# Max unpooling on one core: the load of x issued from ACT's queue instead of SP's

## The chip, the cores and the metric

The kernel runs on one core of a Trainium2 chip. The metric is the device time of one execution in microseconds (us), measured from outside the program; a profiled execution also has a span, the time from its first to its last recorded instruction. Less is better.

The engines that matter here are VectorE (DVE in the profile), which computes, SyncE (SP), which issues DMAs and waits, ScalarE (ACT), which in this kernel computes nothing, and the core's sixteen DMA engines, which carry all transfers between the chip's main memory (HBM) and the on-chip memory (SBUF).

## The reference

Each input value goes to one of the four places of a 2 x 2 block of the output, chosen by its index; the other three are zero.

```python
batch, channels, h, w = 16, 64, 32, 32      # x float32, indices 0..3
output = np.zeros((batch, channels, 2 * h, 2 * w), dtype=np.float32)
for b, c, i, j in all_of(x):
    idx = indices[b, c, i, j]
    output[b, c, 2 * i + idx // 2, 2 * j + idx % 2] = x[b, c, i, j]
```

x has 4.19 MB, the output 16.78 MB. The indices come to the device as 64-bit integers, 8.39 MB; the kernel reads the low 32 bits of each.

## The kernel before

The 1024 images (batch times channels) of 32 x 32 values are laid out so that each of the 128 partitions holds `T = 8` whole images one after another, which in HBM are one contiguous run for each partition. Everything fits into SBUF at once: `x_t` (32 KB a partition), `idx_t` (64 KB) and the output in groups of `G = 2` images (32 KB a partition), `NG = 4` groups in all. The fourth group uses the first group's buffer again (L94).

There are seven DMAs, each over all 128 partitions. Three are loads: the first three images' indices (L110, 24 KB a partition, `cut` marks their end), all of x (L114, 32 KB), and the other five images' indices (L116, 40 KB). Four are stores, one for each group (L151, 32 KB). Before the change all seven are issued from SP.

The order of work is written out by hand. The class `Program` puts instructions into the program's opening block: `first` places a DMA before the first drain of the engine that issues it, so that the loads go out before the engines' opening barrier, each engine's in the order of the calls; `last` moves SP's closing wait to the end of the program.

VectorE waits for x (L121) and for the first indices (L126, again before image 3 for the second indices). Then for each of the four places of the block it runs one instruction (L138) that compares the indices with the place's number and multiplies by x; the result goes with stride two into the output tile, so that the four instructions fill all of it, zeros included. The images 0 to 3 are done one at a time (instructions of 1024 elements a partition), the images 4 and 5, and 6 and 7, in pairs (2048 elements). The last instruction of a group raises the semaphore `made`, on which SP waits before it issues the group's store (L150, L151). Before the fourth group VectorE waits for the first store to have landed (L133). SP waits for the last three stores at the end (L156).

The four instructions of one image or pair:

```python
for pidx in range(4):
    op = nc.vector.scalar_tensor_tensor(
        out=o_c[:, k : k + n, :, pidx // 2, :, pidx % 2],
        in0=idx_c[:, t : t + n], scalar=pidx, in1=x_c[:, t : t + n],
        op0=mybir.AluOpType.is_equal, op1=mybir.AluOpType.mult,
    )
```

Of the kernel before, what the change touches and what calls it, by code (L numbers as in the profile page):

```python
# [1 line left out]

# [4 lines left out]

P = 128
F32 = mybir.dt.float32
I32 = mybir.dt.int32  # L10


class Program:

    def __init__(self, nc):
        self.nc = nc
        self.block = nc.main_func.blocks[0]  # L20
        self.kernel_block = nc.cur_bb.bb.name

    def __enter__(self):
        ins = self.block.instructions
        self.branches = [i for i in ins if "Branch" in type(i).__name__]
        n = len(ins) - len(self.branches)
        assert all("Branch" in type(ins[k]).__name__ for k in range(n, len(ins)))
        del ins[n:]
        self.nc.switch_bb(self.block.name, parent=None)
        self.symbolic = self.nc._always_lower_symbolic_ap  # L30
        self.nc._always_lower_symbolic_ap = False
        return self

    def first(self, made):
        ins = self.block.instructions
        assert ins[len(ins) - 1].name == made.ins.name
        moved = ins.pop()
        at = next(
            k
            for k, i in enumerate(ins)  # L40
            if i.engine == moved.engine and isinstance(i, mybir.InstDrain)
        )
        ins.insert(at, moved)

    def last(self, made):


        def move(nc):
            ins = self.block.instructions
            at = next(k for k, i in enumerate(ins) if i.name == made.ins.name)  # L50
            nc.main_func.blocks[-1].instructions.append(ins.pop(at))

        self.nc.at_finalize(move)

    def __exit__(self, kind, *_):
        self.nc._always_lower_symbolic_ap = self.symbolic
        if kind is None:
            for b in self.branches:
                self.block.instructions.append(b)
            self.nc.switch_bb(self.kernel_block, parent=None)  # L60


@with_exitstack
def kernel(
    ctx: ExitStack,
    tc: tile.TileContext,
    x: bass.AP,
    indices: bass.AP,
    kernel_size: bass.AP,
    out: bass.AP,  # L70
):
    nc = tc.nc
    assert kernel_size == 2

    B, C, H, W = x.shape
    n_img = B * C
    T = n_img // P
    assert T * P == n_img and C % T == 0

    G = 2  # L80
    NG = T // G
    FIRST = 3
    N = H * W
    x_v = x.rearrange("b (ch t) h w -> (b ch) (t h w)", t=T)
    idx_v = indices.rearrange("b (ch t) h w -> (b ch) (t h w)", t=T).bitcast(I32)
    out_v = out.rearrange("b (ch g t) oh ow -> g (b ch) (t oh ow)", g=NG, t=G)

    x_t = nc.alloc_sbuf_tensor("x_t", [P, T * N], F32).ap()
    idx_t = nc.alloc_sbuf_tensor("idx_t", [P, T * 2 * N], I32).ap()
    out_t = [  # L90
        nc.alloc_sbuf_tensor(f"out_t{g}", [P, G * 4 * N], F32).ap()
        for g in range(NG - 1)
    ]
    out_t.append(out_t[0])  # L94

    x_in = nc.alloc_semaphore("x_in")
    idx_in = [nc.alloc_semaphore(f"idx_in{g}") for g in range(2)]
    made = nc.alloc_semaphore("made")
    stored_0 = nc.alloc_semaphore("stored_0")
    stored = nc.alloc_semaphore("stored")  # L100

    x_c = x_t.rearrange("p (t i j) -> p t i j", t=T, j=W)
    idx_c = idx_t.rearrange("p (t i j two) -> p t i j two", t=T, j=W, two=2)[
        :, :, :, :, 0
    ]
    cut = FIRST * 2 * N

    with Program(nc) as program:
        program.first(
            nc.sync.dma_start(out=idx_t[:, :cut], in_=idx_v[:, :cut]).then_inc(  # L110
                idx_in[0], 16
            )
        )
        program.first(nc.sync.dma_start(out=x_t, in_=x_v).then_inc(x_in, 16))  # L114
        program.first(
            nc.sync.dma_start(out=idx_t[:, cut:], in_=idx_v[:, cut:]).then_inc(  # L116
                idx_in[1], 16
            )
        )

        nc.vector.wait_ge(x_in, 16).then_inc(x_in, -16)  # L121
        for t in range(T):
            g, k = t // G, t % G
            if t in (0, FIRST):
                half = int(t == FIRST)
                nc.vector.wait_ge(idx_in[half], 16).then_inc(idx_in[half], -16)  # L126


            if k == 1 and t != FIRST and g:
                continue  # L130
            n = 1 if k == 1 or t + 1 == FIRST or not g else 2
            if g == NG - 1:
                nc.vector.wait_ge(stored_0, 16).then_inc(stored_0, -16)  # L133
            o_c = out_t[g].rearrange(
                "p (m i two j wo) -> p m i two j wo", m=G, two=2, wo=2, j=W
# [4 lines that stand above are left out]
                    in0=idx_c[:, t : t + n],  # L140
                    scalar=pidx,
                    in1=x_c[:, t : t + n],
                    op0=mybir.AluOpType.is_equal,
                    op1=mybir.AluOpType.mult,
                )
            if k + n == G:
                op.then_inc(made, 1)

        for g in range(NG):
            nc.sync.wait_ge(made, g + 1)  # L150
            nc.sync.dma_start(out=out_v[g], in_=out_t[g]).then_inc(  # L151
                stored if g else stored_0, 16
            )
        nc.sync.sem_inc(made, -NG)
        program.last(
            nc.sync.wait_ge(stored, 16 * (NG - 1)).then_inc(stored, -16 * (NG - 1))  # L156
        )


# [1 line left out]
_INS = ['x', 'indices', 'kernel_size']  # L161
_OUTS = [((16, 64, 64, 64), 'float32')]

_NUMBERS = {'kernel_size': 2}


# [26 lines left out]
```

## Time and profile before

| | |
|---|---|
| Median of 9 runs | 71.44 us (71.39 to 71.62) |
| The profiled execution's own time | 71.43 us |
| Its span | 70.1 us |
| VectorE busy | 35.9 us, 24 instructions |
| DMA | 29.36 MB (12.58 MB read from HBM, 16.78 MB written), mean 419 GB/s over the span |
| VectorE, 1024 elements a partition | 16 instructions, 1.22 us each |
| VectorE, 2048 elements a partition | 8 instructions, 2.30 us each |

Times in the profile are microseconds from the span's start. "SPq" stands for SP's sequencer, which issues DMAs and waits; an issue's own length is the time on the sequencer, not that of the transfer. The time "to landing" of a DMA runs from its issue until the last of its sixteen completion marks has arrived, and so includes the time that it stood behind other transfers. In a table of stretches, a DMA packet counts with its whole length where it begins, so that a short stretch can show a share over 1.

### The profile page before, as it was taken

To read this page: it belongs to the slowest core of one execution; us is meant where nothing else is said; L and a number is where in the kernel's file an instruction comes from. 1 tells how busy PE (TensorE), PEld (TensorE's weight loads), DVE (VectorE), ACT (ScalarE), POOL (GpSimd) and SP (SyncE) were. 2 spreads that over 40 slices of the span, in tenths; PEclk is the share of its full clock that TensorE was granted. 3 is DMA by queue.
4 is the path that set the end of the run, shared out by engine and by line. 5 is a ranking of instruction groups with operands and counts; after the bars stand their busy time and mean duration, and the time that the engine had idled before them with its cause. 6 is when DMAs were issued, how large, how long until landed. Compare 5 with 4: busy or idle time off the path is not lost.

```text
span 70.1 us, 76 instructions
## 1 busy us (share of the span) xinstructions
DVE 35.9 (51%) x24; POOL 0.2 (0%) x4
## 2 busy tenths in 40 slices
DVE  0000000000089999999999999999999600000000
POOL 1000000000000000000000000000000000000000
DMA  8699996999988899869999696969999796969893
GB/s 224 294 393 435 449 598 299 505 393 449 524 374 374 374 561 561 374 299 505 393 393 505 299 598 299 598 299 505 393 430 467 318 580 299 598 299 524 374 449 150
DMA packets 1008, 29.36 MB, mean 419 GB/s; under 512 B 112, under 2 KB 112, under 8 KB 112
## 3 DMA queue, kind: packets, MB, share of 16 engines
q1 hardware_dynamic: 1008, 29.36, 97.8%
HBM read 12.58 MB, written 16.78 MB: 419 GB/s over the span
## 4 chain that ended last, share of the span: by engine, by line
DVE 46%; DVEq 4%; issue 1%
DVE out_t L138 46%; DVEq L188 4%
## 5 line engine op out<-in xcount | busy, mean ns | idle before, releaser
L138 DVE SCALAR_TENSOR_TENSOR out_t<-idx_t,x_t 128x1024 f32<-128x1024 int32 (+1 forms) x24 | 35.9, 1580 | 19.5 <-DVEq L126 19.5
L174 POOL MEMSET const-bfloat16-1.0<- 128x1 bf16 x1 | 0.1, 102 | 0.0
L174 POOL MEMSET const-uint8-127<- 128x1 uint8 x1 | 0.1, 102 | 0.0
L174 POOL MEMSET const-float32-0.0<- 128x1 f32 x1 | 0.1, 99 | 0.2 <-issue 0.2
L174 POOL MEMSET const-float32-1.0<- 128x1 f32 x1 | 0.1, 99 | 0.0
## 6 DMA issues: line engine op xcount, KB each, us to landing
out_dram<-out_t SPq DMA_DIRECT2D x4, 4096.0 KB, 13.4
idx_t<-in_indices_dram SPq DMA_DIRECT2D x1, 5120.0 KB, 30.5
x_t<-in_x_dram SPq DMA_DIRECT2D x1, 4096.0 KB, 18.9
idx_t<-in_indices_dram SPq DMA_DIRECT2D x1, 3072.0 KB, 9.6
```

Source lines behind the costliest of these rows:

```text
L138: op = nc.vector.scalar_tensor_tensor(out=o_c[:, k : k + n, :, pidx // 2, :, pidx % 2], in0=idx_c[:, t : t + n], scalar=pidx, in1=x_c[:, t ...
L174: nc = _bacc.Bacc("TRN2", target_bir_lowering=False, num_devices=1)
L188: with _tile.TileContext(nc) as tc:
```

## The change

The DMA that loads x is issued from ACT's queue. The two loads of indices and the four stores stay on SP's queue, in the same order as before. ACT's issue is placed, like SP's, before the engine's first drain; no wait and no semaphore changes, and nothing of VectorE's work.

```diff
         program.first(nc.sync.dma_start(out=idx_t[:, :cut], in_=idx_v[:, :cut]).then_inc(idx_in[0], 16))
-        program.first(nc.sync.dma_start(out=x_t, in_=x_v).then_inc(x_in, 16))
+        program.first(nc.scalar.dma_start(out=x_t, in_=x_v).then_inc(x_in, 16))
         program.first(nc.sync.dma_start(out=idx_t[:, cut:], in_=idx_v[:, cut:]).then_inc(idx_in[1], 16))
```

SP's issues are then: first indices, second indices, four stores. ACT's only issue is x.

## Prediction

> **What bounds the kernel now.** I read the page first, then the timeline, then the DMA issues with their times to landing, first all together and then store by store, then the DMA work in quarter-microsecond stretches at the start, and last the waits.
>
> The page says which resource is full:
>
> ```profile
> span 70.1 us, 76 instructions
> ...
> DVE 35.9 (51%) x24; POOL 0.2 (0%) x4
> ...
> DMA packets 1008, 29.36 MB, mean 419 GB/s; under 512 B 112, under 2 KB 112, under 8 KB 112
> ...
> q1 hardware_dynamic: 1008, 29.36, 97.8%
> ```
>
> VectorE works half of the span; the sixteen DMA engines are at 97.8% of it, all on one queue. The packets also tell the grain of the transfers. There are seven DMAs; 1008 packets less the 112 small ones (16 a DMA, the completion writes) leave 896, that is 128 a DMA: one packet for each partition's row, eight rows a DMA on each engine.
>
> The timeline gives the order of issue (columns: start, length, engine, line):
>
> ```profile
> 0.00 0.38 SPq L110 DMA_DIRECT2D idx_t<-in_indices_dram  x1
> ...
> 0.43 0.42 SPq L114 DMA_DIRECT2D x_t<-in_x_dram  x1
> 0.89 0.43 SPq L116 DMA_DIRECT2D idx_t<-in_indices_dram  x1
> 19.53 35.88 DVE L138 SCALAR_TENSOR_TENSOR out_t<-idx_t,x_t 128x1024 f32<-128x1024 int32 x24 [19.53 <-DVEq L126]
> 28.73 27.03 SPq L151 DMA_DIRECT2D out_dram<-out_t  x4
> ```
>
> The page's DMA issues give the time from issue to landing in their last column:
>
> ```profile
> idx_t<-in_indices_dram SPq DMA_DIRECT2D x1, 5120.0 KB, 30.5
> x_t<-in_x_dram SPq DMA_DIRECT2D x1, 4096.0 KB, 18.9
> idx_t<-in_indices_dram SPq DMA_DIRECT2D x1, 3072.0 KB, 9.6
> ```
>
> and the same view over the stretch of 28 to 30 us gives the first store alone:
>
> ```profile
> out_dram<-out_t SPq DMA_DIRECT2D x1, 4096.0 KB, 12.4
> ```
>
> Issue plus time to landing: the first indices land at 9.6, x at 0.43 + 18.9 = 19.3, the other indices at 0.89 + 30.5 = 31.4, the first store at 28.73 + 12.4 = 41.1. The same view puts the other stores, issued at 37.81, 46.62 and 55.43, at 13.0, 13.8 and 14.6, so they land at 50.8, 60.4 and 70.0. The differences are the price list: 9.7 us for x (1.21 a row on an engine), 12.1 for the second indices (1.51 a row), 9.7 a store. The first indices are three fifths of the second: 0.91 a row, 7.3 in all. Each transfer lands exactly one transfer's time after the one before. Nothing is between them: the kernel is a single file of 7.3 + 9.7 + 12.1 + 4 x 9.7 = 67.9 us, with 2.2 us of start and end, and VectorE matters only where it leaves that file without a next transfer.
>
> The DMA work at the start, in short stretches (the last two columns are DMA share and GB/s of the packets that begin there):
>
> ```profile
> 0.75:1.00 0.25, 0.00 (x0) 0.00 (x0) 1.00 0.00 0
> 1.00:1.25 0.25, 0.00 (x0) 0.00 (x0) 1.00 4.14 1081
> 1.25:1.50 0.25, 0.00 (x0) 0.00 (x0) 1.00 1.73 492
> ```
>
> The first rows begin 1.0 to 1.5 us after the issue, not on all engines at once.
>
> **The handover that matters.** The one place with little room is from loads to stores. VectorE waits for x (L121) and then for the first indices (L126):
>
> ```profile
> DVE out_t L138 <- DVEq L126: 19.5, 1, 19.5
> ```
>
> It starts at 19.53, makes the first output tile in eight instructions of 1.22 us that overlap slightly, and SP issues the first store at 28.73, 9.2 us later. A DMA from issue to landing costs 9.6 - 7.3 = 2.3 us beside its rows. The first store could have landed by itself at 28.73 + 2.3 + 9.7 = 40.7; it landed at 41.1. So the room is 0.4 us by that row. The other bound is the start row: its first packet could begin at 28.73 + 1.0 = 29.7, and the loads land at 31.4, so the room is 1.7 at most. I take 1.0, about the middle, because the 2.3 holds a first read that a busy engine may well hide in part. The later stores have more: 50.8 - (37.81 + 2.3 + 9.7) = 1.0 by the narrow row, then 1.8, then 2.6.
>
> **The change part by part.** One issue of 0.42 us leaves SP's file. SP is then free earlier: the second indices are issued at about 0.43 instead of 0.89, which is worth nothing, as they wait for two transfers on the engines; the cover is 19 us deep. The other steps that SP reaches earlier (the opening barrier) hide under VectorE's wait until 19.5 as well. ACT gains one issue; it has no other work in this kernel, nothing is queued behind it but barriers, and the price of its issue is bounded by SP's 0.38 to 0.43, all hidden. No VectorE instruction moves, no wait is added, no byte is added: 29.36 MB at the rows' prices stay 67.9 us.
>
> What really changes is the order on the engines. Before, x stood behind all of the first indices and ahead of all of the second. Now x has a queue of its own beside SP's, where both index loads follow each other. Two queues with work share an engine, and the trace of before, with one queue, doesn't show how. Bounds: if the rows alternate one by one from the start, eight rows of indices and eight of x end together, at the same 19.3: cost nothing. If x begins after SP's second row has been taken, its last row or completion write stands behind one row of the second indices: 1.51 us later. If the two share bytes evenly, x lands when twice its 4.19 MB has passed, 8.39 MB instead of 7.34 MB: 1.05 MB more at 9.7 us per 4.19 MB, 2.4 us later. Two rows of lag: 3.0 later. I take one row: the first rows begin over a spread of 0.5 us, ACT's issue must arrive on all sixteen engines ahead of SP's second row, and VectorE waits for the last of the sixteen; one engine on which x trails is enough.
>
> [...]
>
> The sum for one row of lag: x lands at 20.8, VectorE starts at 21.0, the first store is issued at 30.2, and the file has a hole of 1.51 less the room of 1.0 = 0.5 us (nothing to 1.1 by the bounds of the room). Nothing gives it back: each store follows the one before without a gap. Nor does it grow: the second store would be issued at 39.3 and has its own room of 1.0 plus the hole of 0.5; the reuse of the first output buffer (L133) waits for the first store's landing at 41.6, and VectorE gets there at 46.5 + 1.5. The second indices still land by 31.4, before VectorE asks at 33.5. So 71.43 + 0.5 = 71.9 us. The profiled execution's 71.43 is its span of 70.1 and 1.3 around it, and lies within 0.01 of the median of the nine runs.
>
> **The rivals.** *Even alternation, not slower:* row by row from the first, x at 19.3, no hole: 71.43, 71.3 to 71.6 with small shifts at the start. For it: the equal number of rows, eight and eight, and packets that are single rows. The decider is whether x's first row is there before SP's second is taken, on every engine. That the two queues are served a whole DMA at a time, so that the change changes no order at all, gives the same time. [...]
>
> *A larger lag:* even bytes or two rows. Delay 2.4 to 3.0, less the room of 0.4 to 1.7: hole 0.7 to 2.6, at the middle 1.4 for even bytes and 2.0 for two rows; 72.1 to 74.0, most likely 72.9. For it: ACT may come late; against it: its first instruction of any kind is at 0.1 us in the trace.
>
> *Faster:* the file can't shrink, but its start can. Engines begin between 1.0 and 1.5 us; if a second queue feeds the late ones sooner, up to 0.5 goes: about 71.15. Against it: the very first row must still be issued and read.
>
> **How the numbers follow.** About 0.2%, 0.14 us, is what a measurement of this kernel can tell from no change. One row of lag 0.36 (its own range 71.6 to 72.5), even alternation 0.30, larger lag 0.22, faster start 0.12. Slower is the first and third and 0.02 of the even case: 0.60. Faster is the last and 0.03 of the even case: 0.15. Same is the remaining 0.25. The range 71.2 to 73.2 leaves out the deepest gains of the start and the upper part of the larger lag, about 0.12 together, and takes in both bounds of the room for one row.
>
> **What would show it.** In the changed profile: x's landing (start of the first VectorE instruction, 19.5 now): 21 for the forecast, 19.5 for the even case, 22 or more for a larger lag. The first indices should land near 17 to 19 instead of 9.6, or the queues don't alternate at all. The first store's landing minus that of the second indices: 9.7 with no hole, 10.2 by the forecast. VectorE's sum stays 35.9. The prediction is wrong if VectorE starts late and the time stays (the room was larger), or if the rows' prices change with two queues, which would show as loads that land together later than 31.4.

## The result and the profile after

The changed kernel takes 71.96 us (median of 10 runs, 71.57 to 72.13) against 71.45 for the kernel before, measured beside it (31 runs, 71.36 to 71.70). The ratio, taken from the means of the runs, is 1.0062, with a 95% interval of 1.0052 to 1.0073: slower by 0.6%, or about 0.5 us. The profiled execution of the changed kernel took 72.13, of which 70.8 are its span; it is the longest of the ten, so its terms below add up to 0.7 and not to 0.5.

The page of the changed kernel, as far as it answers to the lines shown of before (queues: packets, MB, share of sixteen engines; issues: KB and us to landing):

```profile
span 70.8 us, 76 instructions
...
q1 hardware_dynamic: 864, 25.17, 83.3%
q10 hardware_dynamic: 144, 4.19, 13.8%
...
out_dram<-out_t SPq DMA_DIRECT2D x4, 4096.0 KB, 12.3
idx_t<-in_indices_dram SPq DMA_DIRECT2D x1, 5120.0 KB, 31.2
x_t<-in_x_dram ACTq DMA_DIRECT2D x1, 4096.0 KB, 20.9
idx_t<-in_indices_dram SPq DMA_DIRECT2D x1, 3072.0 KB, 18.3
```

The same packets are now on two queues, and their shares add up to 97.1% where one queue had 97.8%. The first indices take 18.3 us to land instead of 9.6: they no longer go ahead of x but beside it. The timeline says what that does to VectorE and the stores:

```profile
0.00 0.38 SPq L110 DMA_DIRECT2D idx_t<-in_indices_dram  x1
0.12 0.37 ACTq L114 DMA_DIRECT2D x_t<-in_x_dram  x1
...
0.43 0.42 SPq L116 DMA_DIRECT2D idx_t<-in_indices_dram  x1
21.24 35.87 DVE L138 SCALAR_TENSOR_TENSOR out_t<-idx_t,x_t 128x1024 f32<-128x1024 int32 x24 [21.24 <-DVEq L126]
30.44 27.03 SPq L151 DMA_DIRECT2D out_dram<-out_t  x4
```

x lands at 0.12 + 20.9 = 21.0, VectorE starts at 21.24 instead of 19.53, and the first store is issued at 30.44 instead of 28.73: everything that VectorE makes is 1.71 late, with its own work unchanged.

**The order of the rows.** Short stretches of the start show it, because rows have three sizes. One row on each of sixteen engines is 0.393 MB for the first indices, 0.524 for x, 0.655 for the second indices. The bytes that begin in a stretch are its length (second column) times its GB/s (last column):

```profile
0.90:2.20 1.30, 0.00 (x0) 0.00 (x0) 1.00 1.09 302
2.20:3.10 0.90, 0.00 (x0) 0.00 (x0) 1.00 1.01 437
3.10:4.20 1.10, 0.00 (x0) 0.00 (x0) 1.00 1.14 477
4.20:5.30 1.10, 0.00 (x0) 0.00 (x0) 1.00 0.83 357
5.30:6.20 0.90, 0.00 (x0) 0.00 (x0) 1.00 1.35 583
```

0.393, 0.393, 0.525, 0.393, 0.525: indices, indices, x, indices, x. In these stretches the two queues take turns row by row, sixteen rows of one kind and then sixteen of the other, and x trails by one row. What that costs shows at the other end of x:

```profile
17.25:18.25 1.00, 0.00 (x0) 0.00 (x0) 1.00 1.22 524
18.25:19.50 1.25, 0.00 (x0) 0.00 (x0) 1.00 1.21 524
```

0.524 MB, then 0.655: x's last sixteen rows, then the first sixteen of the second indices. x's last rows begin by 18.25 and are 1.22 us long, and yet x has landed only at 21.0, about when the rows of the second indices end (begun by 19.5, 1.5 us long). So its completion writes, the small packets at the end of a DMA, sixteen a DMA, stand behind that row: of packets under 512 B on ACT's queue none begins from 18.25 to 19.5, and all sixteen begin from 19.5 to 21.1.

**The hole.** Where the loads end, the kernel before and the changed kernel, each in the same two stretches:

```profile
30.50:31.25 0.75, 0.75 (x2) 0.00 (x0) 1.00 1.63 699
31.25:31.50 0.25, 0.25 (x1) 0.00 (x0) 1.00 0.00 0
```

```profile
30.50:31.25 0.75, 0.75 (x1) 0.00 (x0) 1.00 0.01 0
31.25:31.50 0.25, 0.25 (x2) 0.00 (x0) 1.00 4.86 2097
```

Both have sixteen store rows (0.52 MB) to begin here. Before, each engine begins its row as its last load row ends, spread over 30.5 to 31.25. After, none begins until 31.25, and then all sixteen follow within a quarter of a microsecond: the engines waited for a store that had been issued at 30.44. In stretches of a tenth of a microsecond the sixteen rows begin at 30.8 on average before and at 31.3 after, while the last load rows begin at 29.3 in both: a hole of 0.5 us on the average engine.

### The profile page after: what moved, and what is told of

Its sections match the earlier page's. It is cut to its first block, busy times and chain, and to the rows that moved or that the text cites. A ratio compares the mean times of both kernels' runs of the same rounds, so it can differ in the third digit from the quotient of the medians.

```text
span 70.8 us, 76 instructions
## 1 busy us (share of the span) xinstructions
DVE 35.9 (51%) x24; POOL 0.2 (0%) x4
## 3 DMA queue, kind: packets, MB, share of 16 engines
q10 hardware_dynamic: 144, 4.19, 13.8%
## 4 chain that ended last, share of the span: by engine, by line
DVE 46%; DVEq 3%; issue 1%
DVE out_t L138 46%; DVEq L188 3%
## 5 line engine op out<-in xcount | busy, mean ns | idle before, releaser
L138 DVE SCALAR_TENSOR_TENSOR out_t<-idx_t,x_t 128x1024 f32<-128x1024 int32 (+1 forms) x24 | 35.9, 1582 | 21.2 <-DVEq L126 21.2
## 6 DMA issues: line engine op xcount, KB each, us to landing
out_dram<-out_t SPq DMA_DIRECT2D x4, 4096.0 KB, 12.3
x_t<-in_x_dram ACTq DMA_DIRECT2D x1, 4096.0 KB, 20.9
idx_t<-in_indices_dram SPq DMA_DIRECT2D x1, 3072.0 KB, 18.3
```

The costliest lines, as they stand in the source:

```text
L138: op = nc.vector.scalar_tensor_tensor(out=o_c[:, k : k + n, :, pidx // 2, :, pidx % 2], in0=idx_c[:, t : t + n], scalar=pidx, in1=x_c[:, t ...
```

## Experiments

Each time is given with that of the kernel before, measured beside it on the same chip. The times are medians; the ratio and its 95% interval come from the single runs and can differ a little from the quotient of the medians.

**Was it two queues as such, or what stands behind x?** The second indices move to ACT's queue too:

```diff
-            nc.sync.dma_start(out=idx_t[:, cut:], in_=idx_v[:, cut:]).then_inc(
+            nc.scalar.dma_start(out=idx_t[:, cut:], in_=idx_v[:, cut:]).then_inc(
```

> x and the second indices from ACT's queue, the first indices and the stores from SP's. Theory (rows of two queues take turns, x trails by one row, and the loss comes only from the second indices' row that goes between x's last row and its completion write): now nothing stands behind the first indices on SP's queue, so x lands at about 19.4 instead of 20.9 although it still trails by one row, VectorE starts near 19.6, and the time is that of before, 71.45 (71.3 to 71.6). Rival (a second queue costs by itself, through its issue or through alternation): 71.9 to 72.0 as in the changed kernel.

72.37 against 71.52; ratio 1.0119 (1.0100 to 1.0138). Half of the expectation held: the rows begin as in the changed kernel (0.393, 0.393, then 0.525 MB), x trails, and yet x lands at 0.12 + 19.4 = 19.5. The rows around x's end fit those of the changed kernel (in the page's two slices of 1.77 us from 16.0 to 19.5, 535 and 424 GB/s begin here, 537 and 426 there); but x and the second indices now share a queue, in which x's completion writes stand ahead of the second indices. So the 1.5 us of x come from that one row. The time was a miss, and not by the rival's 71.9 to 72.0 either. The loss sits elsewhere: the first store, issued at 28.97, now comes from SP's queue while ACT's still holds the last load row. The share column of a stretch in which only first store rows begin, times its length, gives the mean length of a row (sixteen rows on sixteen engines). The kernel before, then this run:

```profile
30.50:31.50 1.00, 1.00 (x2) 0.00 (x0) 1.00 1.22 524
```

```profile
30.50:31.50 1.00, 1.00 (x2) 0.00 (x0) 1.00 1.91 524
```

The same bytes, 1.22 us a row before and 1.91 here; that and loads that land at 0.56 + 31.1 = 31.7 instead of 31.4 make up the loss. To see whether the two queues at the start are needed for that, all three loads went to ACT, in the old order, with the stores on SP:

```diff
-nc.sync.dma_start(out=idx_t[:, :cut], ...)     # and x_t, and idx_t[:, cut:]
+nc.scalar.dma_start(out=idx_t[:, :cut], ...)   # and x_t, and idx_t[:, cut:]
```

> All three loads from ACT's queue in the old order, the four stores from SP's. No two queues share the engines until the first store comes. Theory: the start costs nothing more than in the kernel before, x lands at 19.4 to 19.5, no hole; but the first store's row and the loads' last row now come from two queues at the handover, which in the run with x and the second indices on ACT made the first store's rows 2.0 to 2.2 us long instead of 1.21; so 72.1 to 72.4. Rival (that loss came from the two queues at the start): 71.45 to 71.6.

72.40 against 71.48; ratio 1.0128 (1.0115 to 1.0142). VectorE starts at 19.7, the loads land at 1.01 + 30.6 = 31.6, and the stretch from 30.5 to 31.5 has a share of 1.60 for the same 0.524 MB: the longer first store rows at a handover between two queues need no sharing at the start. They are 0.4 us of the 0.9 lost (the expectation's 2.0 to 2.2 us for the run before is 1.91 in the view above), and the later landing of the loads is another 0.2. The changed kernel doesn't pay for longer rows: its stores follow the second indices on SP's own queue, and its first store rows took 1.22 us (0.25 x 4.86, the view above).

**The mirror image:** the first indices from ACT, x and the second indices from SP.

```diff
-            nc.sync.dma_start(out=idx_t[:, :cut], in_=idx_v[:, :cut]).then_inc(
+            nc.scalar.dma_start(out=idx_t[:, :cut], in_=idx_v[:, :cut]).then_inc(
```

> The mirror image: the first indices from ACT's queue, x and the second indices from SP's. Theory: now the first indices trail by one row and their completion write stands behind a row of the second indices; they land at about 20.9, x near 18, VectorE starts near 21.2, and the time is 71.9 to 72.0. Rival (ACT's queue is slow for x's large rows alone, or x is special): VectorE starts near 19.5 and the time is 71.45.

71.71 against 71.52; ratio 1.0025 (1.0015 to 1.0034). A miss that teaches. The start of this run:

```profile
0.90:2.60 1.70, 0.00 (x0) 0.00 (x0) 1.00 1.15 308
2.60:3.60 1.00, 0.00 (x0) 0.00 (x0) 1.00 0.92 393
```

0.524 MB, then 0.393: x, indices. ACT's first sixteen rows took the second turn, and nothing trailed; why, one profile doesn't show. x landed at 19.6, the first indices at 0.12 + 19.7 = 19.8, and the first store, issued at 29.16, landed at 41.4, 9.7 after the loads (31.7): no hole. This is the even alternation of the rivals, and it shows what two queues cost here without a lag: the loads land 0.3 later than before, and the time is 0.2 longer.

**Do turns go by rows or by bytes?** x in two DMAs of half rows on ACT (the edit is shown against the kernel before):

```diff
-        program.first(nc.sync.dma_start(out=x_t, in_=x_v).then_inc(x_in, 16))
+        half_x = T * N // 2
+        for lo in (0, half_x):
+            program.first(nc.scalar.dma_start(
+                out=x_t[:, lo : lo + half_x], in_=x_v[:, lo : lo + half_x]).then_inc(x_in, 16))
...
-        nc.vector.wait_ge(x_in, 16).then_inc(x_in, -16)
+        nc.vector.wait_ge(x_in, 32).then_inc(x_in, -32)
```

> The changed kernel with x loaded by two DMAs of half rows (16 KB) from ACT's queue: sixteen rows an engine against eight of the first indices. VectorE waits for both. Theory (queues take turns row by row, whatever the rows' size): x's last eight rows take turns with the second indices' eight, so x lands only near 31.3, with all loads; VectorE starts near 31.5, the first store is issued near 40.7, the DMA engines stand empty for about 10.6 us, and the time is about 82. Rival (queues share bytes evenly): the size of rows does not matter, x lands at 20 to 22 and the time is 71.9 to 72.9.

82.64 against 71.53; ratio 1.155. From the timeline of this run:

```profile
31.79 35.87 DVE L144 SCALAR_TENSOR_TENSOR out_t<-idx_t,x_t 128x1024 f32<-128x1024 int32 x24 [31.79 <-DVEq L132]
40.99 27.03 SPq L157 DMA_DIRECT2D out_dram<-out_t  x4
```

The bytes are the same, the number of rows is doubled, and VectorE, which waits for x, starts only when all loads have landed. Even bytes are refuted, and the hole costs what it measures: the first store is 12.3 us later than in the kernel before, less a room of about one, and the time is 11.1 longer.

The opposite, the first indices in two DMAs of half rows on SP (two issues of `cut // 2` elements, and the wait at L126 for 32 instead of 16):

> The changed kernel with the first indices loaded by two DMAs of half rows (12 KB) from SP's queue: sixteen rows ahead of the second indices. Theory (turns row by row): x takes turns with the first eight to ten of these rows and lands near 15 to 16, the first indices end at 19.2 with nothing between, VectorE starts near 19.5, time 71.45 (71.3 to 71.6). Rival (even bytes): x still shares with the second indices and lands at 20.9 or later, time 71.9 or more.

71.90 against 71.53; ratio 1.0055 (1.0042 to 1.0068). x lands early, at 0.12 + 16.9 = 17.0, as row turns demand; VectorE starts at 19.90 and the first store is issued at 29.09, no later than the mirror image's 29.16, which left no hole. But the loads land at 0.89 + 31.0 = 31.9, half a microsecond later than before. Of that the start has about 0.3, an estimate from the stretches: the 1.88 MB that begin here from 0.9 to 6.2 us took 5.27 us an engine, the 1.64 MB of the kernel before from 0.9 to 5.3 took 4.39, and the 0.24 MB between would take 0.55 at its 9.7 us for 4.19 MB. The later landing covers the time's 0.4. The expectation of 71.45 had no term for a start with two queues.

**The room at the first store, by itself.** One queue, and one or two extra VectorE instructions into a spare buffer ahead of the first:

```diff
+            for s in spare if t == 0 else []:      # one buffer, or two
+                nc.vector.scalar_tensor_tensor(
+                    out=s.rearrange("p (m i j) -> p m i j", m=1, j=W), in0=idx_c[:, :1],
+                    scalar=0, in1=x_c[:, :1],
+                    op0=mybir.AluOpType.is_equal, op1=mybir.AluOpType.mult)
```

> The kernel before, one queue, with one extra VectorE instruction of 1.14 us into a spare buffer ahead of the first, so that everything VectorE makes comes 1.14 later. It measures the room at the first store. Theory (room about 1.3, since a store's first row begins 0.9 after its issue and the loads' rows end near 31.0): 71.45 to 71.6. By the narrow room of 0.4: 72.15. By the wide room of 1.7: 71.45.

> The same with two extra instructions, 2.27 us. Theory (room about 1.3): hole of 1.0, time 72.4. By the narrow room of 0.4: 73.3. By the wide room of 1.7: 72.0. With the changed kernel's delay of 1.7 between the two runs, its 71.96 should lie on the line between them.

One: 71.63 against 71.53; ratio 1.0019 (1.0010 to 1.0028), with the first store issued at 29.88. Two: 72.77; ratio 1.0171 (1.0157 to 1.0185), issued at 31.00. A delay of 2.27 costs 1.24, so the room is 1.0. In the second run the same picture as in the changed kernel, one step later:

```profile
31.25:31.50 0.25, 0.25 (x1) 0.00 (x0) 1.00 0.00 0
31.50:32.00 0.50, 0.50 (x1) 0.00 (x0) 1.00 2.44 1049
```

Here too the first store rows begin 0.8 to 1.0 us after the issue. The changed kernel's issue at 30.44 lies between the two. A straight line between their profiled executions (71.56 us at 29.88, 72.69 at 31.00) gives 71.56 + 0.56 / 1.12 x 1.13 = 72.12 for it, and the changed kernel's profiled execution took 72.13. So the late issue alone, with one queue, gives that execution's time to within the 0.1 by which the kernel before differs between the two sets of runs. The line of the medians gives 72.2, above the changed kernel's median of 71.96; when its other executions issued the store isn't known, as only the longest has a profile.

**Taking the hole away.** The first store goes out in parts, so that VectorE's late start leaves no hole: first in two halves, for the changed kernel and for the kernel before.

```diff
-            if k + n == G:
+            if k + n == G or not g:
                 op.then_inc(made, 1)
...
+        for k in range(G):                         # the first group's store, image by image
+            nc.sync.wait_ge(made, k + 1)
+            nc.sync.dma_start(out=out_v[0][:, k * image : (k + 1) * image],
+                in_=out_t[0][:, k * image : (k + 1) * image]).then_inc(stored_0, 16)
```

> The changed kernel, with the first store issued in two halves, each as soon as its image is made. Theory: x still lands at 20.9 and VectorE still starts at 21.2, but the first half-store is issued near 25.9, four us before the loads end, so the hole after the loads is gone and the time is 71.45 to 71.6. Rival (the loss lies in the loads: slower rows or a slower start with two queues): still 71.9 to 72.0.

> The control to the run before: one queue, first store in two halves. Theory: there was no hole to fill, 71.45 (71.35 to 71.6). If halving the store gains or costs by itself, it shows here: by the rival that halves are worth something in themselves, 71.2 or 71.7.

Both miss by far: 72.89 and 72.91 against 71.52 (ratios 1.0186, 1.0167 to 1.0204, and 1.0198, 1.0177 to 1.0218). The control shows that this loss needs no second queue. The kernel before, then its version with two halves, in the stretch in which each engine begins its last load row:

```profile
29.00:30.50 1.50, 1.50 (x2) 0.00 (x0) 1.00 1.01 437
```

```profile
29.00:30.50 1.50, 1.50 (x2) 0.00 (x0) 1.00 1.74 437
```

1.5 x 1.01 = 1.52 us a row before, 1.5 x 1.74 = 2.61 with half a store, issued at 24.32, waiting behind it. Before that row the one of 27.5 to 29.0 is 0.3 us longer than in the kernel before (shares of 1.01 and 1.19), and the two together are the 1.4 us that this version loses. So the handover seems to have two edges: too late leaves a hole, too early slows the last load rows. These two runs alone don't tell an early issue from the cut itself. Two more cuts of the first store, in the second image, put its first part between these edges: after 20 of the image's 32 rows, in both kernels, and after 24 in the changed one.

```diff
+            parts = [slice(0, ROWS), slice(ROWS, H)] if t == 1 else [slice(0, H)]
+            for rows in parts:
...
+        cuts = [0, 4 * N + 4 * ROWS * W, G * 4 * N]
```

> The changed kernel with the first store in two parts again, but the first part now ends in the middle of the second image (20 of its 32 rows), so that VectorE has it ready about 28.8, as in the kernel before, instead of 25.8. Theory A (the hole after the loads is the changed kernel's loss, and a store that is issued about 2.5 us before the loads end costs them nothing): x still lands near 20.9, VectorE starts near 21.2, no hole, loads end near 31.5 to 31.7, time 71.5 to 71.7. Theory B (halving the first store is what costs, whenever it is issued): 72.5 or more, with slow last rows of the loads as in the run with two halves.

> The same cut in the kernel before, one queue: the first part is ready about 27.1, 4.3 us before the loads end. Theory A (a store that waits behind loads for more than a row of theirs slows their last rows): between the two known points, no loss at an issue of 28.7 and 1.4 at 24.3, so 71.8 to 72.6, with slow loads rows from 29 us on. Theory B (halving costs): 72.5 or more. If the kernel before was only lucky by a little, 71.5.

> As the run with the cut at 20 rows of the second image, but at 24 rows, so that the first part is ready about 0.4 us later. In the run with 20 rows the times fell into two groups, 71.5 to 71.7 and 72.5 to 72.7, and its profile, of the second group, shows x without a lag (landed 19.6), so that the first part was issued at 27.5, too early. Theory (two orders of the first rows, with and without a lag of x): with the lag, the first part is issued near 29.2, no hole, loads end near 31.5 to 31.6, time 71.5 to 71.7, while VectorE starts at 21.2; without the lag, it is issued near 27.9 and the time lies between 71.6 (if the loss of an early store ends there) and 72.5. The time then falls into two groups again, and the group with the lag is the faster one. Rival (the lag of x itself costs, apart from the hole): no run under 71.8 with VectorE's start at 21.2.

One queue, 20 rows: first part issued at 27.2, 72.82 against 71.48 (ratio 1.0188, 1.0171 to 1.0204); slow last rows again (share 1.67 from 29.0 to 30.5, or 2.5 us a row). That is a little over the range of theory A and within that of theory B, so this run doesn't decide between them. The changed kernel with 20 rows fell into two groups, seven times from 71.54 to 71.73 and four from 72.51 to 72.66, with a median of 71.67 (ratio 1.0048, 1.0012 to 1.0083). Its profile is of the slower group and begins thus:

```profile
0.90:2.20 1.30, 0.00 (x0) 0.00 (x0) 1.00 1.23 302
2.20:3.10 0.90, 0.00 (x0) 0.00 (x0) 1.00 1.35 583
```

0.393, then 0.525: the same loads, but this time x took the second turn. With x at 19.6 the part was issued at 27.46, too early, and the last load rows took 1.5 x 1.57 = 2.36 us. Theory B, by which the cut costs whenever it is issued, doesn't fit the seven times under 71.8 of the same kernel. With 24 rows the times again fall apart: nine runs from 71.48 to 71.80, two at 72.10 and 72.25, the median 71.59 against 71.53 (ratio 1.0017, 1.0000 to 1.0034). Its profile is the 72.25 one, without a lag, issued at 27.95, and its last load rows took 1.5 x 1.36 = 2.04 us. In the profiles of the kernels cut in the second image the last load row gets shorter as the issue gets later: 2.5 us at 27.2, 2.36 at 27.46, 2.04 at 27.95, and the uncut store, issued at 28.73, has 1.52. The order is that of the issue, but the size of the first part differs too. The faster groups fit the forecast for the order with the lag and no hole, but no profile of them was taken, so that their order is inferred and not shown. None of these versions beats the kernel before.

The one-queue runs sort by the time of the first store's issue: 24.3 costs 1.4 us, 27.2 costs 1.3, 28.73 nothing, 29.88 costs 0.1, 31.00 costs 1.24.

## Why the prediction was right

- *The bound.* Held. VectorE's work is 35.9 us in both, and its late start matters only through the hole.
- *The lag of one row.* Held in the profile of the changed kernel, for all sixteen first rows, by the order of the rows; landing of x 21.0 for a forecast of 20.8, VectorE's start 21.24 for 21.0, first store 30.44 for 30.2. Of the 1.71 us of delay, 1.5 are one row of the second indices, as the run shows that took that row away (x at 19.5 with the same lag). The other 0.2 are not in the sum. That the lag came at all was in part luck: it had a chance of 0.36, and the same loads gave the other order in two profiles with a cut first store. The 71.57 among the ten runs may be such an execution; no profile shows it.
- *The room of 1.0.* Held: 2.27 of delay cost 1.24 with one queue. It lies between the bounds of 0.4 and 1.7. The prediction took about their middle and no row gave it the value, so that it fits so closely is in part luck too. What the 2.3 us beside a transfer's rows is made of, a first read or anything else, no run shows.
- *The hole of 0.5.* Right for the average engine, by the store rows above. The sum for the profiled execution is 1.71 of delay less 1.0 of room, 0.7, which is what that execution lost. Seen by landings, that is 0.2 for the loads (31.6 instead of 31.4), 0.2 for the first store behind them (30.44 + 11.1 = 41.5 instead of 41.1) and 0.3 for the three other stores, which take 29.2 us from there instead of 28.9; with the one-queue delay of 2.27 they take 29.2 as well.
- *The signs it named.* x and the first indices landed as forecast (21.0 and 18.3). The first store landed 9.9 after the second indices, between the 10.2 of the forecast and the 9.7 of no hole: a landing shows the last engine of each transfer, and there the hole is smaller than on the average one. And the loads landed later than 31.4, which the prediction had called a sign of being wrong: with two queues from the start they landed at 31.6, 0.2 later, a term that the sum put at nothing. The median came out at the forecast's 0.5 without it; which of its terms were smaller in the executions without a profile is not known. One reading is off without effect: VectorE's first instruction on the second indices starts at 33.2 before and 34.9 after, not at 33.5.
- *The price of ACT's issue.* Held: 0.37 us, beside one of SP's of 0.38 that had begun 0.12 earlier; no wait is seen in these lengths.
- *A whole DMA at a time.* Refuted: the turns here are single rows (0.393, 0.393, 0.525, 0.393, 0.525 MB for sixteen), and the first indices landed at 18.3 instead of 9.6.
- *Even bytes.* Refuted by 82.64 us with half rows. *Even alternation* was real, in the mirror image, where it cost 0.2 and not nothing, and in the two profiles without a lag. *A faster start* was seen nowhere: in no run has the last load landed before 31.4.

## What to carry to other kernels

Where transfers already fill the DMA engines, as here, a second queue added no bandwidth (415 GB/s over the span instead of 419); it changed who goes first. Ask which load the next engine waits for, count the rows of each queue rather than the bytes, and look at what stands behind the short queue: one row of a third transfer was 1.5 of the 1.7 us of delay here. Then measure the room at each handover by delaying the producer a known amount, before you trust that a microsecond of delay will hide.

## What was unexpected of the hardware

A store that waits behind loads can, it seems, be too early. Issued 1.5 to 4.4 us sooner than in the kernel before, with one queue, its first part lengthened the loads' last rows from 1.52 to as much as 2.61 us and cost 1.3 to 1.4 us, with the same bytes in the same queue. The store was cut in two in all of these runs; an uncut store issued as early was not run. With the last loads and the first store on different queues the first store rows took 1.6 to 1.9 us instead of 1.22, at nearly the same time of issue (28.9 to 29.0 against 28.7). Why a waiting store should slow the loads in front of it, and why the first store rows are longer with two queues, is not settled by these runs.

The order of the first rows between two queues issued 0.12 us apart is not fixed: for one and the same set of loads both orders were profiled (the second sixteen rows are 0.393 MB in the changed kernel and 0.525 in the two with its first store cut in the second image).
